# Hidden units and their sums swap storage after the first turn of a Strassen-like MLP, and their stores are split over two stages

## The chip, the cores and the metric

The kernel runs on one core of one Trainium2 chip. The metric is the device time of one execution in microseconds (us), as the median of some runs. All times inside an execution are counted from the start of the profiled span. Engines are called by their profile names: PE (matrix multiply), ACT (scalar engine), DVE (vector engine), POOL (GpSimd) and SP, which here only issues DMAs, in order, from one queue.

## The reference, cut to what matters

The program is one layer of an encoder: a mixer of two attention kinds, a cross-attention, and an MLP with a squared ReLU. Only the MLP is touched here. With 1024 tokens, a model width of 1024 and a hidden width of 4096 it computes

```python
h = h + parallel_mixer(...)
h = h + memory_cross_attention(...)
u = jax.nn.relu(rms_norm(h, norm_mlp_g) @ mlp_w1)    # (1024, 1024) @ (1024, 4096)
h = h + (u * u) @ mlp_w2                              # (1024, 4096) @ (4096, 1024)
```

## The kernel before, in words

All matrix products are in float32 precision: every operand is split into a high part and a low part, and one product is three matmuls (lines L107, L108 and L109, in `gemm`). Inside the MLP the kernel also uses a seven-product scheme for 2x2 block matrices (Winograd's form of Strassen's method): seven block products instead of eight, paid with sums and differences of blocks. A **stage** is one of these seven block products; it is done for two block rows, `i` = 0 and 1, each with 12 matmuls of 128x512 when four 128-deep slices are contracted. So a stage is 24 matmuls.

The MLP has two parts.

The **hidden part** (`mlp`, the loop over `p`) makes the squared units in eight **turns** of seven stages. A turn makes two units groups, q = 2p + i. What a group leaves is eight planes of 128x512: four planes of units, called `c` (c[0] to c[3]), and four planes of sums and differences of them, called `t` (t[0] to t[3]). They live for the length of a turn in the storage of the state `h`, seen as `h4` with four blocks of four planes: `h4[:, 2 + i]` holds `c` and `h4[:, i]` holds `t`. The function `hidden(i, j, ps)` takes the PSUM bank of stage `j`: stages 0 to 2 are copied by ACT (L1151), stages 3 to 5 are added by DVE (L1159). At stage 5 ACT applies ReLU and square to c[0:3] (L1161, L1162) and DVE forms t[0:3] (L1163, L1164); at stage 6 ACT makes c[3] (L1153, L1154) and DVE makes t[3] (L1156). Then two DMAs of 1 MB each store c (L1155) and t (L1157) into `ud[q]` in DRAM, planes 0 to 3 and 4 to 7.

The **output part** (the loop over `CHUNKS`) reads the planes of `nk` groups back from `ud` (L1202), splits them (ACT L1203, DVE L1204), multiplies them with blocks of `w2` and accumulates into `h`, which is free by then. It goes over `o` = 0 and 2: with o = 0 the function `output` writes rows k = 0 to 3 of `h`, which is the storage of `h4` blocks 0 and 1; with o = 2 it writes blocks 2 and 3. In the first chunk the stages j = 0, 2, 3 and 6 are plain copies by ACT (L1228), the others are DVE adds (L1230). A copy may write into `h` only when the DMA that stores the old content of these planes has landed. In the first chunk's seven stages, j = 2 and j = 4 and 6 accumulate in the same PSUM bank as j = 0, and j = 5 in the bank of j = 3, so the matmuls of j = 2 wait until ACT has read the bank of j = 0.

The weights are loaded by `weights7` into a pool `raw7` of two buffers (SP, L1060), split by ACT and DVE (L1039, L1040), and summed into tiles `s` by POOL in the output part (L1065, L1066, L1072, L1073). Names in the traces and listings: `x_1859`, `x_1896`, `x_1860`, `x_1908`, `x_1899`, `x_1909` and `x_1910` are the seven operand tiles of the hidden stages 0 to 6, reused as slots for what the output part reads back; `my`, `mm` and `tr` are PSUM banks; `g` is a split weight.

The order of the instructions on each engine is made by a scheduler when the program is built, from the dependences between tiles and its own estimates. A change of the code in one place can so reorder others.

Of the kernel before, what the change touches and what calls it, by code (L numbers as in the profile page):

```python
# [51 lines left out]
class Layer:  # L52
# [1041 lines left out]
    def mlp(self, mx):  # L1094
        nc = self.nc
# [15 lines left out]
        def prep(*args):  # L1111
            w = self.weights7(*args)
            A = next(w)
            next(w)
            return A
# [25 lines left out]
        h4 = h.rearrange("p k s -> p (k s)").rearrange("p (b c s) -> p b c s", b=4, s=512)  # L1141
        for p in range(NQ // 2):
            if p:
                A = prep([self.w1[2 * p + i] for i in range(2)], 512, nc.vector, True)

            def hidden(i, j, ps):

                c, t, q = h4[:, 2 + i], h4[:, i], 2 * p + i
                v = c[:, (0, 2, 1, 1, 2, 0, 3)[j]]
                if j in (0, 1, 2):  # L1150
                    nc.scalar.activation(v, ps, AF.Copy)  # L1151
                elif j == 6:
                    nc.scalar.activation(v, ps, AF.Relu)  # L1153
                    nc.scalar.activation(v, v, AF.Square)  # L1154
                    nc.sync.dma_start(self.ud[q, :, 0:4, :], c)  # L1155
                    nc.vector.tensor_tensor(t[:, 3], v, t[:, 2], ALU.subtract)  # L1156
                    nc.sync.dma_start(self.ud[q, :, 4:8, :], t)  # L1157
                else:
                    nc.vector.tensor_tensor(v, ps, v, ALU.add)  # L1159
                    if j == 5:  # L1160
                        nc.scalar.activation(c[:, 0:3], c[:, 0:3], AF.Relu)  # L1161
                        nc.scalar.activation(c[:, 0:3], c[:, 0:3], AF.Square)  # L1162
                        nc.vector.tensor_tensor(t[:, 0:2], c[:, 1:3], c[:, 0:2], ALU.subtract)  # L1163
                        nc.vector.tensor_tensor(t[:, 2], c[:, 2], t[:, 0], ALU.subtract)  # L1164

            def taken(i, j, ps):
                hidden(i, j, ps)
                if p == 0 and i == 1:
                    next(turn, None)

            self.products7(self.HIDDEN, A, B, 4, taken)
            if p == 1:

                self.token_squares(0, self.yv[:, 0:4])
                nc.vector.reciprocal(self.yv, self.yv)
                nc.vector.tensor_tensor(self.yv, self.yv, self.hv, ALU.mult)
            if p == 3:
                F = self.T(self.s7, [P, 2, 512], F32, "s7")
                for half in range(2):
                    ps = next(self.banks)  # L1180
                    self.spread(ps, self.smallp, self.yv[:, 4 * half:4 * half + 4])
                    nc.scalar.activation(F[:, half], ps, AF.Copy)
                nc.sync.dma_start(self.fd, F)
# [12 lines left out]
        for nk in CHUNKS:  # L1196
            B = {}
            for names, room, which in groups:
                for q in range(q0, q0 + nk):
                    t = room[q % 4]  # L1200
# [91 lines left out]
```

## Time and profile before

| What | Value |
|---|---|
| median of the runs | 1480.72 us (1478.56, 1480.72, 1490.71) |
| the profiled execution's own time | 1479.95 us |
| its span | 1478.2 us |
| PE busy | 1428.4 us, 97% of the span |
| DVE, ACT, POOL busy | 925.1, 683.1, 431.8 us |
| MLP | about 851 us to the end |
| last hidden turn | about 1120 to 1158 us |

The span is what the trace covers; 1.75 us of the execution's time lie outside of it. The busy share of PE says that it nearly always has a matmul in flight, not that it runs at its peak. What a change can win must therefore be looked for in the places where PE waits.

### The profile page before, as it was taken

The numbers are of one execution on the slowest core, as the hardware profiler recorded it, in microseconds if no ns is written. First come the engines' busy times: TensorE is split into PE (matmuls) and PEld (weight loads), VectorE is DVE, ScalarE is ACT, GpSimd is POOL, SyncE is SP. The second block draws the span as 40 slices with busy tenths as digits, with TensorE's granted clock in tenths as the row PEclk, the third lists the DMA queues.
The fourth block names the chain that finished last, engine by engine and source line by source line (L and its number), as shares of the span: only waits on it lengthen the run. The fifth ranks groups of instructions, "written<-read, shape, count | busy, mean of one in ns | idle before, by whom it ended". The sixth has DMA issues, their size and how long they took to land.

```text
span 1478.2 us, 19169 instructions
## 1 busy us (share of the span) xinstructions
PE 1428.4 (97%) x7058; PEld 1193.7 (81%) x7058; DVE 925.1 (63%) x1323; ACT 683.1 (46%) x1095; POOL 431.8 (29%) x457
## 2 busy tenths in 40 slices
PE   8998999998998998999999999999999899999998
PEld 6777888886887787888888878888888688888886
DVE  4386422427776576666654895647556939688686
ACT  4474332326776555445542264445445626335230
POOL 2157503323473312622212300000000523333454
PEclk9999999999999999999999999999999999999999
DMA  8425530258677642503375114444446827337353
GB/s 269 126 51 124 143 86 1 72 176 249 183 207 200 190 156 72 161 31 114 117 269 191 45 65 171 171 171 185 171 171 234 280 71 240 129 109 232 115 200 114
DMA packets 125118, 223.94 MB, mean 151 GB/s; under 512 B 8384, under 2 KB 66528, under 8 KB 118368
## 3 DMA queue, kind: packets, MB, share of 16 engines
q1 hardware_dynamic: 125024, 222.71, 46.6%
q8 instruction: 56, 0.92, 0.3%
q14 instruction: 38, 0.31, 0.1%
HBM read 150.59 MB, written 72.09 MB: 151 GB/s over the span
## 4 chain that ended last, share of the span: by engine, by line
PE 80%; DMA 8%; DVE 6%; ACT 2%; issue 2%; POOL 1%; SPq 0%; POOLq 0%; ACTq 0%; DVEq 0%
PE mm L107 13%; PE mm L108 13%; PE mm L109 13%; PE my L108 7%; PE my L107 7%; PE my L109 7%; PE tr L108 3%; PE tr L107 3%; PE tr L109 3%; DMA raw<-in_w_in_dram 1%; PE tr L661 1%; DMA raw<-in_xattn_wkv_dram 1%; PE pv L668 1%; PE pv L669 1%; PE s L621 1%
## 5 line engine op out<-in xcount | busy, mean ns | idle before, releaser
L107 PE MATMUL my<-x,g 128*128 128x512 f32 x464 | 181.5, 392 | 6.4 <-ACT h L1228 6.4
L108 PE MATMUL my<-x,g 128*128 128x512 f32 x464 | 181.6, 391 | 1.3 <-DVE x L1040 1.3
L109 PE MATMUL my<-x,g 128*128 128x512 f32 x464 | 181.1, 391 | 0.0
L108 PE MATMUL mm<-wl,xh 128*128 128x512 f32 x320 | 126.0, 395 | 3.6 <-DVE wl L97 3.6
L107 PE MATMUL mm<-wh,xh 128*128 128x512 f32 x320 | 126.9, 399 | 0.8 <-ACT gv L485 0.8
L1040 DVE TENSOR_TENSOR g<-raw,g 128x1024 fp32r<-128x1024 f32 (+3 forms) x72 | 66.9, 931 | 96.7 <-ACT g L1039 96.7
L109 PE MATMUL mm<-wh,xl 128*128 128x512 f32 x320 | 125.8, 394 | 0.0
L1039 ACT ACTIVATE g<-s 128x1024 fp32r<-128x1024 f32 (+1 forms) x72 | 69.0, 963 | 119.4 <-PE my L109 51.5
L1065 POOL TENSOR_TENSOR s<-raw 128x384 f32<-128x384 f32 (+1 forms) x20 | 26.2, 1312 | 298.1 <-DMA raw<-in_mlp_w_dram 268.9
L107 PEld LDWEIGHTS my<-x,g 128*128 128x128 f32 x464 | 87.6, 189 | 25.1 <-ACT h L1228 6.9
L108 PEld LDWEIGHTS my<-x,g 128*128 128x128 f32 x464 | 87.7, 189 | 19.7 <-DVE x L1040 1.7
L109 PEld LDWEIGHTS my<-x,g 128*128 128x128 f32 x464 | 87.6, 189 | 18.4 <-DVE g L1040 0.2
L1039 ACT ACTIVATE g<-raw 128x1024 fp32r<-128x1024 f32 (+3 forms) x72 | 55.4, 773 | 98.6 <-PE my L109 36.2
L1040 DVE TENSOR_TENSOR g<-s,g 128x1024 fp32r<-128x1024 f32 (+1 forms) x72 | 84.8, 1180 | 14.5 <-ACT g L1039 14.4
L632 POOL TENSOR_SCALAR p<-p,rrec 128x128 f32<-128x128 f32 (+3 forms) x64 | 50.6, 793 | 128.0 <-DVE rrec L631 121.7
L107 PE MATMUL mm<-x,g 128*128 128x512 f32 x220 | 85.7, 390 | 0.0
L108 PE MATMUL mm<-x,g 128*128 128x512 f32 x220 | 85.7, 389 | 0.0
L109 PE MATMUL mm<-x,g 128*128 128x512 f32 x220 | 85.6, 389 | 0.0
L109 PE MATMUL tr<-x,g 128*128 128x512 f32 x212 | 82.6, 390 | 0.3 <-DVE g L1040 0.3
L107 PE MATMUL tr<-x,g 128*128 128x512 f32 x212 | 82.5, 389 | 0.0
L108 PE MATMUL tr<-x,g 128*128 128x512 f32 x212 | 82.5, 389 | 0.0
L1204 DVE TENSOR_TENSOR x<-x 128x1024 fp32r<-128x1024 f32 (+1 forms) x64 | 78.6, 1247 | 6.0 <-ACT x L1203 5.8
(313 smaller groups left out, 3764.6 us busy)
## 6 DMA issues: line engine op xcount, KB each, us to landing
ud<-h SPq DMA_DIRECT2D x32, 1024.0 KB
x<-ud SPq DMA_DIRECT2D x48, 512.0 KB
raw<-in_mlp_w_dram SPq DMA_DIRECT2D x20, 1024.0 KB
raw<-in_mlp_w_dram SPq DMA_DIRECT2D x16, 768.0 KB
raw<-in_w_in_dram SPq DMA_DIRECT2D x23, 512.0 KB
raw<-in_xattn_wkv_dram SPq DMA_DIRECT2D x16, 512.0 KB
od<-o SPq DMA_DIRECT2D x32, 256.0 KB
xt<-in_x_dram SPq DMA_DIRECT2D x8, 512.0 KB
```

The costliest lines, as they stand in the source:

```text
L107: mm(ps, lh[k], rh[k], start=start and k == 0, stop=False, **kw)
L108: mm(ps, lh[k], rl[k], start=False, stop=False, **kw)
L109: mm(ps, ll[k], rh[k], start=False, stop=stop and k == n - 1, **kw)
L621: nc.tensor.matmul(ps[:, c], qa[:, ts], ka[:, c], start=True, stop=False)
L632: nc.gpsimd.tensor_scalar(p[:, 0:n], p[:, 0:n], rr, 1.0, ALU.mult, ALU.mult)
L661: nc.tensor.transpose(o, pp[i][:, kb * P:(kb + 1) * P], self.ident)
L668: nc.tensor.matmul(pv, va[:, kb, :], th[:, js], start=kb == 0, stop=False)
L669: nc.tensor.matmul(pv, va[:, kb, :], tl[:, js], start=False, stop=kb == nb - 1)
L1039: self.nc.scalar.activation(hi, src, AF.Copy)
L1040: self.nc.vector.tensor_tensor(lo, src, f(hi), ALU.subtract)
L1065: eng.tensor_tensor(s[:, 0], raw[:, 3], raw[:, 2], ALU.add)
L1204: nc.vector.tensor_tensor(lo, f(lo), f(hi), ALU.subtract)
```

## The change

```diff
             def hidden(i, j, ps):

-                c, t, q = h4[:, 2 + i], h4[:, i], 2 * p + i
+                c, t = (h4[:, b] for b in ((2 + i, i) if p == 0 else (i, 2 + i)))
+                q = 2 * p + i
                 v = c[:, (0, 2, 1, 1, 2, 0, 3)[j]]
                 if j in (0, 1, 2):
                     nc.scalar.activation(v, ps, AF.Copy)
                 elif j == 6:
                     nc.scalar.activation(v, ps, AF.Relu)
                     nc.scalar.activation(v, v, AF.Square)
-                    nc.sync.dma_start(self.ud[q, :, 0:4, :], c)
+                    nc.sync.dma_start(self.ud[q, :, 3, :], v)
                     nc.vector.tensor_tensor(t[:, 3], v, t[:, 2], ALU.subtract)
-                    nc.sync.dma_start(self.ud[q, :, 4:8, :], t)
+                    nc.sync.dma_start(self.ud[q, :, 7, :], t[:, 3])
                 else:
                     nc.vector.tensor_tensor(v, ps, v, ALU.add)
                     if j == 5:
...
                         nc.scalar.activation(c[:, 0:3], c[:, 0:3], AF.Square)
                         nc.vector.tensor_tensor(t[:, 0:2], c[:, 1:3], c[:, 0:2], ALU.subtract)
                         nc.vector.tensor_tensor(t[:, 2], c[:, 2], t[:, 0], ALU.subtract)
+                        for r, src in ((0, c), (4, t)):
+                            nc.sync.dma_start(self.ud[q, :, r:r + 3, :], src[:, 0:3])
```

It does two things. From the second turn on, the units `c` stand in blocks 0 and 1 of the storage and the sums `t` in blocks 2 and 3. And each of the two stores of 1 MB is divided: planes 0 to 2 (768 KB) go out at stage 5, when they are complete, and the last plane (256 KB) at stage 6. Each turn issues eight stores instead of four; the bytes are the same. No arithmetic is added or removed. Lines behind the change are numbered three higher, so the ACT copy L1228 becomes L1231 and L1202 becomes L1205. The new store of three planes is L1167; those of single planes are L1156 (c) and L1158 (t).

The first place is the queue of SP at the end of the last turn. Its rows before, from the load of the third weight block of the output part to the first load of the next chunk; `raw` is a weight buffer, `x` a slot that is filled from `ud`:

```order
L1060 DMA raw_2086_10811<-in_mlp_w_dram 128x4x512
L1202 DMA x_1910_8688<-ud_68 128x512 x2
L1060 DMA raw_2088_10816<-in_mlp_w_dram 128x4x512
L1155 DMA ud_68<-h_5812 128x2048
L1157 DMA ud_68<-h_5812 128x2048
L1155 DMA ud_68<-h_5812 128x2048
L1157 DMA ud_68<-h_5812 128x2048
L1060 DMA raw_2106_11075<-in_mlp_w_dram 128x4x384
```

And now:

```order
L1060 DMA raw_2086_10843<-in_mlp_w_dram 128x4x512
L1205 DMA x_1909_8657<-ud_68 128x2x512 x2
L1167 DMA ud_68<-h_5812 128x1536
L1205 DMA x_1910_8688<-ud_68 128x512 x4
L1167 DMA ud_68<-h_5812 128x1536 x3
L1060 DMA raw_2088_10848<-in_mlp_w_dram 128x4x512
L1156 DMA ud_68<-h_5812 128x512 x2
L1158 DMA ud_68<-h_5812 128x512 x2
L1060 DMA raw_2106_11107<-in_mlp_w_dram 128x4x384
```

The four stores of three planes moved ahead of the load of `raw_2088`, the first of them also ahead of the four loads of `x_1910`; the four stores of one plane stand behind that load, where the whole stores stood. The two loads of `x_1909`, which stood ahead of `raw_2086`, now stand behind it.

The second place is ACT at the start of the output part. `my_2080` and `my_2081` are the banks of stage 0 (and 2) for i = 0 and 1, `tr_2084` and `tr_2085` those of stage 3; the copies L1203 and L1206 split operand slots. Before:

```order
L1203 ACTIVATE x7_1910_8688<-x7_1910_8688 128x512 x2
L1039 ACTIVATE g2_2076_10611<-s7_2074_10605 128x1024
L1039 ACTIVATE g2_2077_10614<-s7_2075_10608 128x1024
L1228 ACTIVATE h_1369_5812<-my_2080_10623 128x512
L1228 ACTIVATE h_1369_5812<-tr_2084_10705 128x512
```

And now:

```order
L1231 ACTIVATE h_1369_5812<-my_2080_10655 128x512
L1206 ACTIVATE x7_1910_8688<-x7_1910_8688 128x512 x4
L1039 ACTIVATE g2_2076_10643<-s7_2074_10637 128x1024
L1039 ACTIVATE g2_2077_10646<-s7_2075_10640 128x1024
L1231 ACTIVATE h_1369_5812<-my_2081_10669 128x512
```

The copy of the bank of stage 0 for i = 0 moved ahead of the splits of `x_1910` and of two weight splits; that for i = 1 stands right behind them.

The third place is PE, where the matmuls of output stage 2 for i = 0 begin. Before, the stages 0, 1 and 3 are all done first, 72 matmuls; the rows around the border:

```order
L108 MATMUL tr_2085_10719<-x7_1908_8628,g2_2073_10602 128x512
L109 MATMUL tr_2085_10719<-x7_1908_8628,g2_2073_10602 128x512
L107 MATMUL my_2080_10623<-x7_1860_8212,g2_2071_10596 128x512
L108 MATMUL my_2080_10623<-x7_1860_8212,g2_2071_10596 128x512
L109 MATMUL my_2080_10623<-x7_1860_8212,g2_2071_10596 128x512
```

And now:

```order
L108 MATMUL tr_2084_10737<-x7_1860_8212,g2_2071_10628 128x512
L109 MATMUL tr_2084_10737<-x7_1860_8212,g2_2071_10628 128x512
L107 MATMUL my_2080_10655<-x7_1860_8212,g2_2071_10628 128x512
L108 MATMUL my_2080_10655<-x7_1860_8212,g2_2071_10628 128x512
L109 MATMUL my_2080_10655<-x7_1860_8212,g2_2071_10628 128x512
```

Stage 2 for i = 0 now begins after 54 matmuls of the output part, in the middle of stage 3 for i = 0, which is 18 matmuls sooner. Behind it come the other six matmuls of that stage, three of stage 3 for i = 1, and then stage 2 for i = 1, so that this begins after 75. Stage 5 for i = 0, the first to use the bank `tr_2084` again, begins after 108.

## The prediction

> **What bounds the kernel now.** I began with the page, then asked who PE waited for in the MLP, then followed the chain of waits there.
>
> ```profile
> span 1478.2 us, 19169 instructions
> ...
> PE 1428.4 (97%) x7058; PEld 1193.7 (81%) x7058; DVE 925.1 (63%) x1323; ACT 683.1 (46%) x1095; POOL 431.8 (29%) x457
> ```
>
> PE is busy for 97% of the span, so a change that adds and removes no matmul can win only where PE stands still. The waits of PE between 850 us and the end (columns: total us, times, longest) are three:
>
> ```profile
> PE my L107 <- ACT h L1228: 6.4, 1, 6.4
> PE my L108 <- DVE x L1040: 1.3, 1, 1.3
> PE tr L109 <- DVE g L1040: 0.3, 1, 0.3
> ```
>
> Only the first is large. The chain of waits (start, length, what) shows what stood behind it:
>
> ```profile
> 1170.68 0.61 DVE h L1156
> 1171.31 9.43 DMA ud<-h
> 1180.83 0.60 ACT h L1228
> 1181.48 0.79 PE my L107
> ```
>
> This is the step from the hidden part to the output part. ACT may not copy output stage 0 into the storage of the state until the sums t of group 14, which lie there, are in DRAM. Their store is issued at 1171.31 and has landed at 1180.7. The timeline of PE shows what that costs:
>
> ```profile
> 1174.65 0.39 PE L109 MATMUL tr<-x,g 128*128 128x512 f32 x1
> 1181.48 0.79 PE L107 MATMUL my<-x,g 128*128 128x512 f32 x1 [6.44 <-ACT h L1228]
> ...
> 1186.51 0.40 PE L107 MATMUL tr<-x,g 128*128 128x512 f32 x1
> ...
> 1188.78 0.39 PE L108 MATMUL tr<-x,g 128*128 128x512 f32 x1
> ```
>
> Undisturbed matmuls start every 0.227 us (ten steps between the last two rows, 2.27 us). The one after 1174.65 should have started at 1174.88 and starts at 1181.48: **6.60 us**. The next 12 then take 1181.48 to 1186.51, 5.03 us instead of 12 x 0.227 = 2.72: another **2.31 us**. The windows give the reason, a granted clock (the figure behind POOL's) of 0.50 after the wait; the last two columns are the share of the DMA engines and GB/s:
>
> ```profile
> 1158.00:1162.00 4.00, 4.00 (x19) 3.22 (x18) 4.00 (x4) 4.00 (x6) 1.91 (x1) 1.00 0.86 249
> 1166.00:1170.00 4.00, 4.00 (x19) 3.32 (x18) 4.00 (x2) 4.00 (x8) 3.00 (x2) 1.00 0.00 0
> 1175.00:1181.00 6.00, 0.04 (x1) 0.00 (x0) 6.00 (x7) 0.17 (x1) 2.43 (x2) 0.86 1.02 431
> 1181.00:1186.00 5.00, 4.52 (x11) 3.56 (x12) 0.69 (x2) 0.92 (x2) 4.83 (x4) 0.50 0.78 328
> ```
>
> The second row is the telling one: from 1166 to 1170 no DMA moves anything, and afterwards they are full. The queue of SP says why:
>
> ```profile
> 1157.70 0.55 SPq L1060 DMA_DIRECT2D raw<-in_mlp_w_dram  x1
> 1158.34 1.04 SPq L1202 DMA_DIRECT2D x<-ud  x2
> 1169.02 0.55 SPq L1060 DMA_DIRECT2D raw<-in_mlp_w_dram  x1
> 1169.67 0.57 SPq L1155 DMA_DIRECT2D ud<-h  x1
> 1171.31 0.32 SPq L1157 DMA_DIRECT2D ud<-h  x1
> 1171.74 0.71 SPq L1155 DMA_DIRECT2D ud<-h  x1
> 1177.56 0.32 SPq L1157 DMA_DIRECT2D ud<-h  x1
> ```
>
> All four stores stand behind a weight load that goes out at 1169.02. POOL holds it, with the last of its sums over the buffer to be reloaded, done at 1168.99:
>
> ```profile
> 1166.71 2.28 POOL L1073 TENSOR_TENSOR s<-raw,s 128x512 f32<-128x512 f32 x1
> ```
>
> Meanwhile the first three planes of the units had long been made (ACT, groups 14 and 15), while the first three planes of group 15's sums were finished late, behind other work of DVE:
>
> ```profile
> 1153.60 1.49 ACT L1162 ACTIVATE h<-h 128x1536 f32<-128x1536 f32 x1
> ...
> 1161.88 1.47 ACT L1162 ACTIVATE h<-h 128x1536 f32<-128x1536 f32 x1
> ```
>
> ```profile
> 1170.01 0.68 DVE L1164 TENSOR_TENSOR h<-h 128x512 f32<-128x512 f32 x1
> ```
>
> **The change, part by part.** *The swap.* Output stage 0 now overwrites the units, which are ready earlier than the sums: 1155.09 for group 14 and 1163.35 for group 15. *The split.* Planes 0 to 2 go out ahead of the late weight load. The first copy needs plane 0 alone, so it waits for the first L1167 only.
>
> When does that store land? At the earliest it is issued when ACT is done, 1155.09; 0.79 MB at 431 GB/s are 1.8 us, so 1156.9. At the latest it goes behind the load at 1157.70 and the two loads of x_1909 that now stand between them. I count these in full: 1.05 + 1.05 + 0.79 = 2.89 MB from 1157.70 on. At 249 GB/s, the rate of the window from 1158 to 1162, that is 11.6 us, so 1169.3; at 431 GB/s it is 6.7 us, so 1164.4. ACT's copy takes 0.60, so the bank is free between 1157.5 and 1169.9. I take some 1165, nearer to the middle, since the earlier stores of the sixth turn also leave less in the queue ahead.
>
> When is it needed? The hidden part ends 71 matmuls and the 0.3 us of the small stall before 1174.65, at 1158.2. Stage 2 for i = 0 now begins after 54 matmuls, 1158.2 + 54 x 0.227 = 1170.5. So even the latest bound is 0.6 us in time, and my value 5 us. For i = 1 ACT has behind the first copy four splits of x_1910, two weight splits and the copy:
>
> ```profile
> 1168.65 1.14 ACT L1203 ACTIVATE x<-x 128x512 fp32r<-128x512 f32 x2
> 1169.69 2.09 ACT L1039 ACTIVATE g<-s 128x1024 fp32r<-128x1024 f32 x2
> ```
>
> That is 2 x 1.14 + 2.09 + 0.60 = 5.0 us, so 1174.9 from the latest bound, and it is needed after 75 matmuls, at 1175.2. Its store, of group 15's units, waits for 1163.35 and moves 0.79 MB behind the 1.05 MB of x_1910: 1.84 MB at 249 GB/s are 7.4 us, so 1170.8.
>
> *The single planes* c[3] stand behind raw_2088, and that now stands behind the sums of group 15, made at 1170.69 in the old order. 0.79 + 1.05 + 0.26 = 2.10 MB then take 4.9 us at 431 GB/s or 8.4 at 249: landed between 1175.6 and 1179.1. Stage 5 for i = 0 needs the copy of stage 3 after 108 matmuls, at 1182.7. This has 3 to 7 us. The sums themselves are now overwritten by o = 2 only, 168 matmuls or 38 us after 1158.2. The weight load raw_2088 may be 2 us later than before; its matmuls begin after 180, at 1199.
>
> *The small stall* of 0.3 us, PE's wait for a weight split on DVE: DVE is behind there, and the operand loads now come earlier, since three quarters of the sixth turn's stores have left. I count it as gone; staying would cost 0.3.
>
> *More DMAs.* Four more issues per turn. A turn's end on SP now looks like this:
>
> ```profile
> 970.76 0.38 SPq L1157 DMA_DIRECT2D ud<-h  x1
> 982.00 0.33 SPq L1060 DMA_DIRECT2D raw<-in_mlp_w_dram  x1
> ```
>
> The next weights go out 11 us after the last store, held by their buffer, so four more issues of 0.3 to 0.9 us are hidden; without that cover they would cost 3 us on that load. In the turns the DMAs have room, and the copies that waited for a store (ACT, 13 times) never held PE:
>
> ```profile
> 889.00:927.00 38.00, 38.00 (x169) 31.48 (x168) 22.18 (x29) 18.66 (x23) 0.00 (x0) 1.00 0.43 166
> ```
>
> ```profile
> ACT h L1151 <- DMA ud<-h: 27.6, 13, 3.4
> ```
>
> With stores at stage 5 those waits only shorten. I cost the turns at nothing; as the other end, 1 us in each of seven turns is 7 us lost.
>
> One rule speaks against the change. The Trainium skill, "DMA: Bandwidth & Descriptors", section "Rules for kernel authors", asks for at least 1 MiB per DMA and to coalesce many small transfers; the change does the opposite. The trace bears out that smaller loads run slower: 249 GB/s around the loads of 256 KB, 431 around whole stores. By that rule the first store lands near 1169.3 in place of 1165, which leaves the sum as it is but little in hand, and speaks for the first rival below.
>
> The sum: 6.60 + 2.31 + 0.3 = **9.2 us** of the profiled execution's 1479.95, so 1470.7, and I say 1471. That execution lies 0.8 us below the median of the runs shown, 1480.72, one of which is 10 us above the others.
>
> **The rivals.** *A part of the wait stays.* If POOL lets raw_2086 go 3 us later, or the loads are slower, the first store lands past 1169.9, and PE waits for the rest. Short waits here also cost clock: earlier in this trace PE waited 1.9 us, and the window behind has a granted clock of 0.59.
>
> ```profile
> PE pv L669 <- DVE ptl L115: 1.9, 1, 1.9
> ```
>
> ```profile
> 554.00:558.00 4.00, 3.78 (x19) 3.32 (x18) 4.00 (x9) 2.56 (x6) 1.17 (x2) 0.59 0.56 193
> ```
>
> A rest of 3 us plus 2 us of half clock leaves 9.2 - 5 = 4 us of gain: 1476. For it: the load stands ahead of the store, and ACT works in order. Against: the latest bound, made of the slowest rate, is still in time. The Trainium skill, "TensorE: Matmul & The Clock Gate", section "Why this matters for your kernels", sets the limit for a clock drop at idle gaps of about 3 us; by it a rest of 2 us would cost no clock and give 1473, while the row with 1.9 us says it may.
>
> *The change does not do what it says.* The stores stay held in SP's queue, or another wait of the same length takes the place, as DVE, 4.00 of 4.00 us busy from 1166 to 1170, is still behind. Then 1480. Against it: neither the first store nor the copy behind it needs DVE's sums.
>
> *Slower.* The single planes c[3] are the place. They stand behind raw_2088, which waits for POOL's sums, for the third store ahead of it and so for DVE. If they land after 1182.1, PE stops at stage 5. From a wait of 9.2 - 2.3 = 6.9 us, that is landing at 1189, 10 us after the slow bound, the kernel is slower than before; a raw_2088 held until 1187 in place of 1171 would land them at some 1194 with the 2.10 MB, a wait of 12 + 2.3 us: 1485. For it: three things in a row that each wait in order. Against: DVE and POOL get their operands earlier, not later.
>
> **How the numbers follow.** Forecast (the wait goes, 1471): 0.67. A part stays (1476): 0.16. No change (1480): 0.08. Slower (1485, with a tail): 0.09. The lower end takes all three waits of PE and the half clock away, 1479.95 - 8.0 - 2.3 = 1469.6, and 1.4 us for runs that differ (1478.56 against 1479.95): 1468. The upper end takes in the cases to no change and a little of the slower one: 1482. About 1%, 14.8 us, is what a measurement of this kernel can tell from no change. A gain above it would need more waits than PE has in the MLP, so faster 0.02; slower by more is the tail of the last rival, 0.04; within 1% 0.94.
>
> **What would show it.** Right: no wait of PE on L1231 near 1170, no window of granted clock 0.50 there, the first L1167 of the last turn issued between 1155 and 1160, DMAs at work between 1166 and 1170, MLP turns still 38 us long. Wrong: PE waiting for L1231 on a bank `my` (first store late) or `tr` (single planes late), or for L1040 inside the turns (weights late), or the granted clock low in another place.

## The result, and the profile after

The changed kernel takes 1476.06 us in the median of 22 runs (1467.45 to 1482.72); the kernel before, in 22 runs beside them, 1484.3 us (1478.56 to 1490.71). The ratio is **0.9947, with a 95% interval from 0.9935 to 0.9959**: a gain of 7.9 us, between 6.1 and 9.6. The profiled execution took 1476.15 us.

The head of its page, span and first section:

```profile
span 1474.3 us, 19250 instructions
...
PE 1427.8 (97%) x7058; PEld 1193.9 (81%) x7058; DVE 927.6 (63%) x1323; ACT 683.4 (46%) x1095; POOL 431.2 (29%) x457
```

The engines' work is what it was; what changed is where PE stands still. Its waits after 850 us:

```profile
PE my L107 <- ACT h L1231: 1.7, 1, 1.7
PE my L108 <- DVE x L1040: 1.3, 1, 1.3
PE my L184 <- DVE dg L183: 1.2, 2, 1.0
```

The 6.4 us before ACT's copy have become 1.7, the small stall on DVE's weight split is gone, and one wait is new, on L184 in a hidden turn. The timeline of PE at the step:

```profile
1173.77 0.39 PE L107 MATMUL my<-x,g 128*128 128x512 f32 x1
...
1178.33 0.39 PE L109 MATMUL tr<-x,g 128*128 128x512 f32 x1
1180.38 0.50 PE L107 MATMUL my<-x,g 128*128 128x512 f32 x1 [1.67 <-ACT h L1231]
...
1183.23 0.39 PE L107 MATMUL tr<-x,g 128*128 128x512 f32 x1
```

Stage 2 for i = 0 begins at 1173.77 without a wait; the wait that is left stands before stage 2 for i = 1. It should have started at 1178.56 and starts at 1180.38, 1.8 us late. The 12 matmuls behind it take 2.85 us, where undisturbed ones take 2.72: no half clock this time. The windows (DMA share and GB/s last, the clock ahead of them) say the same:

```profile
1158.00:1162.00 4.00, 4.00 (x20) 3.30 (x19) 4.00 (x4) 2.74 (x3) 4.00 (x3) 1.00 0.18 46
...
1166.00:1170.00 4.00, 4.00 (x19) 3.30 (x19) 3.97 (x4) 3.64 (x4) 1.02 (x1) 1.00 0.94 344
1175.00:1181.00 6.00, 4.33 (x20) 3.27 (x19) 6.00 (x7) 4.32 (x7) 3.77 (x2) 1.00 1.02 381
1181.00:1186.00 5.00, 5.00 (x24) 4.13 (x23) 5.00 (x7) 1.64 (x3) 1.78 (x2) 1.00 0.69 264
```

The hole in the DMAs from 1166 to 1170, which carried the prediction, is filled. The granted clock is 1.00 in all four. But there is a new hole ahead, from 1158 to 1162. The queue of SP shows it:

```profile
1159.81 0.55 SPq L1060 DMA_DIRECT2D raw<-in_mlp_w_dram  x1
1160.44 1.08 SPq L1205 DMA_DIRECT2D x<-ud  x2
1163.10 0.33 SPq L1167 DMA_DIRECT2D ud<-h  x1
1163.52 2.10 SPq L1205 DMA_DIRECT2D x<-ud  x4
1167.73 4.30 SPq L1167 DMA_DIRECT2D ud<-h  x3
1172.86 0.55 SPq L1060 DMA_DIRECT2D raw<-in_mlp_w_dram  x1
```

The first L1167 goes out at 1163.10, as soon as ACT has made group 14's units. ACT made them late, because it waited 2.44 us for DVE's add at stage 5. DVE made that add at 1158.55, right behind two weight splits; in the kernel before, these two come behind both adds of stage 5 (L1159, at 1151.37 and 1156.44), at 1158.68 and 1161.51. The rows of DVE, then those of ACT:

```profile
1155.21 3.41 DVE L1040 TENSOR_TENSOR g<-raw,g 128x1024 fp32r<-128x1024 f32 x2
1158.55 0.68 DVE L1160 TENSOR_TENSOR h<-my,h 128x512 f32<-128x512 f32 x1
```

```profile
1159.26 1.49 ACT L1162 ACTIVATE h<-h 128x1536 f32<-128x1536 f32 x1 [2.44 <-DVE h L1160]
1160.65 1.04 ACT L1206 ACTIVATE x<-x 128x1024 fp32r<-128x1024 f32 x1
1161.60 1.47 ACT L1163 ACTIVATE h<-h 128x1536 f32<-128x1536 f32 x1
...
1166.72 1.48 ACT L1163 ACTIVATE h<-h 128x1536 f32<-128x1536 f32 x1
...
1172.95 0.58 ACT L1231 ACTIVATE h<-my 128x512 f32<-128x512 f32 x1
...
1179.73 1.09 ACT L1231 ACTIVATE h<-my 128x512 f32<-128x512 f32 x2 [1.68 <-DMA ud<-h]
```

Group 15's units are ready at 1168.20. Their store is issued at 1169.09, when a load of x_1909 has landed, and the chain of waits says how long it then took:

```profile
1160.44 8.58 DMA x<-ud
1169.09 10.56 DMA ud<-h
1179.73 0.61 ACT h L1231
1180.38 0.50 PE my L107
```

10.56 us for 0.79 MB is 75 GB/s, in a stretch in which all DMAs together moved some 380 (381 from 1175 to 1181). It shared the engines with transfers issued beside it, among them the three planes of sums of group 14 (1167.73) and of group 15 (1171.71), which nobody was waiting for.

### The profile page after: what moved, and what is told of

Same layout as the page of the kernel before. It is cut to its first block, busy times and chain, and to the rows that moved or that the text cites. A ratio compares the mean times of both kernels' runs of the same rounds, so it can differ in the third digit from the quotient of the medians.

```text
span 1474.3 us, 19250 instructions
## 1 busy us (share of the span) xinstructions
PE 1427.8 (97%) x7058; PEld 1193.9 (81%) x7058; DVE 927.6 (63%) x1323; ACT 683.4 (46%) x1095; POOL 431.2 (29%) x457
## 4 chain that ended last, share of the span: by engine, by line
PE 66%; issue 16%; DMA 9%; DVE 5%; ACT 2%; POOL 1%; SPq 0%; POOLq 0%; DVEq 0%; ACTq 0%
PE mm L107 12%; PE mm L108 12%; PE mm L109 12%; PE my L108 4%; PE my L107 4%; PE my L109 4%; PE tr L107 2%; PE tr L108 2%; PE tr L109 2%; DMA raw<-in_w_in_dram 2%; PE tr L661 1%; DMA raw<-in_xattn_wkv_dram 1%; PE pv L669 1%; PE pv L668 1%; PE s L621 1%
## 5 line engine op out<-in xcount | busy, mean ns | idle before, releaser
L1040 DVE TENSOR_TENSOR g<-raw,g 128x512 fp32r<-128x512 f32 (+3 forms) x72 | 68.3, 951 | 69.1 <-ACT g L1039 69.0
L1039 ACT ACTIVATE g<-raw 128x512 fp32r<-128x512 f32 (+3 forms) x72 | 55.5, 773 | 101.0 <-DMA raw<-in_mlp_w_dram 39.3
L1040 DVE TENSOR_TENSOR g<-s,g 128x1024 fp32r<-128x1024 f32 (+1 forms) x72 | 86.1, 1199 | 7.7 <-ACT g L1039 7.5
```

Source lines behind the costliest of these rows:

```text
L1039: self.nc.scalar.activation(hi, src, AF.Copy)
L1040: self.nc.vector.tensor_tensor(lo, src, f(hi), ALU.subtract)
```

## The experiments

All times of the MLP in the table are read from the trace: its start is PE's first matmul into a bank `my`, and its length goes from there to the end of the span. "Step" is PE's wait for the copy (L1228 before, L1231 after). A gain in us is worked out from the ratio; plain medians can differ from it by about 1 us.

| kernel | ratio to before (95%) | MLP starts | MLP length | step |
|---|---|---|---|---|
| before, three profiles | | 849.3, 854.4, 856.2 | 628.9, 628.6, 628.6 | 6.4, 6.7, 6.8 |
| whole change, two profiles | 0.9947, 0.9946 | 851.1, 852.1 | 623.2, 623.5 | 1.7, 2.0 |
| split alone, two profiles | 0.9967, 0.9954 | 853.7, 853.3 | 622.6, 623.0 | 1.2, 1.4 |
| swap alone | 0.9983 (0.9968 to 0.9998) | 855.3 | 628.2 | 4.3 |
| swap, units' store split | 0.9940 (0.9919 to 0.9960) | 851.0 | 621.2 | none |
| all turns but the last | 1.0006 (0.9992 to 1.0021) | 852.9 | 629.8 | 6.0 |
| swap, units' store split, spread on POOL | 0.9962 (0.9942 to 0.9983) | 851.2 | 624.1 | none |
| last turn, units' store split | 0.9946 (0.9927 to 0.9964) | 853.3 | 620.3 | none |

**Split alone.** The blocks stay where they were:

```diff
-                c, t = (h4[:, b] for b in ((2 + i, i) if p == 0 else (i, 2 + i)))
+                c, t = h4[:, 2 + i], h4[:, i]
```

> Stores split as in the change, but units and sums keep their old places. The queue of SP has the same order as in the changed kernel. Theory A (both parts are needed): the first ACT copy now waits for the first three planes of the sums of group 14, whose store is issued some 5 us later than that of the units, behind the loads of x_1910; it lands about 4 us too late for PE, PE waits about 4 us for that copy and loses about 2 us more to the half clock. Gain on the kernel before 3 us (1 to 5). Theory B (the split alone does it): no more than the 1.7 us wait of the changed kernel, gain about 8 us. Theory C (the swap alone does it) and theory D (the gain lies in the turns): gain 0 by C, about 8 us by D.

Measured: 1478.88 us, ratio 0.9967 (0.995 to 0.9984), 4.9 us of gain. PE's waits at the step and in the turns:

```profile
PE my L108 <- DVE x L1040: 1.3, 1, 1.3
PE my L184 <- DVE dg L183: 1.2, 2, 1.0
PE my L107 <- ACT h L1231: 1.2, 1, 1.2
```

A is wrong on the mechanism: without the swap the step's wait is 1.2 us, not 4, and there is no half clock. The sums are ready later than the units, but the scheduler answered by putting stage 2 for i = 0 after 68 matmuls of the output part instead of 54, and ACT's copy for it at 1180.16 was nearly in time. The gain of 4.9 us is still inside A's 1 to 5, so the two kernels were measured side by side.

**Whole change and split alone on one chip.**

> The changed kernel itself, on the same chip and in the same rounds as the three kernels that follow, so that they can be compared with it directly. Both theories: 7.9 us faster than before (6.1 to 9.6), a ratio of 0.9947; PE waits 1.7 us for the second copy L1231 and 1.2 us on L184 in a turn, and the granted clock stays at 1.00 behind both.

> The stores divided in all turns, the units and sums not swapped: once more, now beside the whole change. A (the swap is worth something on top of the split): 2 to 4 us slower than the whole change in the same rounds, as the two separate comparisons with before say (4.9 against 7.9 us of gain). B (the split alone is the change): within 1.5 us of it, since both traces show PE waiting the same 1.2 to 1.8 us at the step and 1.2 us on L184, and no half clock.

Measured: the whole change 1476.01 us (1475.23 to 1477.44), ratio 0.9946 (0.9931 to 0.9961); split alone 1478.15 us (1475.55 to 1478.74), ratio 0.9954 (0.9938 to 0.997). The medians differ by 2.1 us, which would be A's, the ratios by 0.0008, which is 1.2 us and would be B's, and the intervals overlap widely; in the MLP itself split alone is the shorter one by 0.5 us. So B stands in the traces, and that the swap is worth anything on top of the split is not shown. The window at the step of this second profile of the whole change, with PE's wait of 2.0 us ending at 1181.63, has a full clock too:

```profile
1181.00:1186.00 5.00, 4.37 (x19) 3.60 (x20) 5.00 (x8) 2.02 (x3) 0.51 (x1) 1.00 0.93 351
```

**Swap alone.** The whole stores at stage 6 come back:

```diff
-                    nc.sync.dma_start(self.ud[q, :, 3, :], v)
+                    nc.sync.dma_start(self.ud[q, :, 0:4, :], c)
...
-                    nc.sync.dma_start(self.ud[q, :, 7, :], t[:, 3])
+                    nc.sync.dma_start(self.ud[q, :, 4:8, :], t)
...
-                        for r, src in ((0, c), (4, t)):
-                            nc.sync.dma_start(self.ud[q, :, r:r + 3, :], src[:, 0:3])
```

> Units and sums swapped after the first turn, but stored whole at the seventh stage. The queue of SP has the same order as in the kernel before. Theory A (both are needed): the store of the units of group 14 still stands behind the weight load held until 1169, but one store of 1 MB ahead of the sums, so it lands 1.05 MB / 0.43 MB per us = 2.4 us sooner; PE still waits about 4 us and has the half clock. Gain on the kernel before 2.4 us (1 to 4). Theory C (the swap alone does it): PE's wait under 2 us, gain about 8 us. Theories B (split alone) and D (turns): gain 0.

Measured: 1481.67 us, ratio 0.9983, 2.5 us of gain, as A said, of which the MLP's length shows 0.5: the step's wait is 2.1 us shorter than in the first profile of before, but a wait for DVE's split (L1040) grows from 0.3 to 0.9 us and the turns are 0.7 us longer. The step keeps its wait and the half clock behind it (waits, the queue of SP, and the window after the step):

```profile
PE my L107 <- ACT h L1229: 4.3, 1, 4.3
```

```profile
1176.29 0.55 SPq L1060 DMA_DIRECT2D raw<-in_mlp_w_dram  x1
1176.93 0.57 SPq L1156 DMA_DIRECT2D ud<-h  x1
```

```profile
1186.00:1192.00 6.00, 5.33 (x13) 4.19 (x14) 2.86 (x3) 1.12 (x3) 4.79 (x4) 0.54 1.02 431
```

The store still goes out right behind the late weight load. Swapping what is waited for helps little while both kinds of planes stand behind the same held load.

**All turns but the last.** Swap and split for p = 1 to 6, split for p = 0, the last turn as before:

```diff
+                split = p < NQ // 2 - 1
+                c, t = (h4[:, b] for b in ((i, 2 + i) if 0 < p < NQ // 2 - 1 else (2 + i, i)))
```

> Swap and split in the turns before the last only; the last turn keeps the old places and whole stores, so the step to the output part is as in the kernel before. Theory A (the gain is all at the step): PE waits 6 to 7 us on the first copy as before and has the half clock; gain 0 (within 1.5 us either way). Theory D (the turns gain): about 8 us.

Measured: 1483.81 us, ratio 1.0006 (0.9992 to 1.0021), with the step back at its old wait:

```profile
PE my L107 <- ACT h L1232: 6.0, 1, 6.0
```

Of the 64 parts into which 32 stores are divided, 56 gain nothing. A holds: the whole gain lies at the one step. The MLP's length is 629.8 against 628.7; the fourth turn (p = 3) is 1.7 us longer, as in the changed kernel, and the step's wait a little shorter.

**Only the units' store divided.** This tests why the second copy was late. The sums of both groups leave whole at stage 6, so they are no longer in the DMA engines beside group 15's units:

```diff
-                    nc.sync.dma_start(self.ud[q, :, 7, :], t[:, 3])
+                    nc.sync.dma_start(self.ud[q, :, 4:8, :], t)
...
-                        for r, src in ((0, c), (4, t)):
+                        for r, src in ((0, c),):
```

> The change, but only the units' store is split; the sums are stored whole at the seventh stage, behind the weight load. Theory A with the rest of the wait put down to the DMA queue (in the changed kernel the units of group 15 land 10.6 us after their issue, with the 0.79 MB of group 14's sums ahead of them): these land 2 us sooner, PE's wait of 1.7 us on L1231 falls under 0.5 us; gain on the kernel before 9 to 10 us, 1.5 us more than the change. Rival: the rest is set by ACT's own order (operand and weight splits ahead of the second copy), then the wait stays between 1.2 and 2 us and the gain is that of the change, 8 us.

Measured: 1474.7 us, ratio 0.9940, 8.9 us of gain, just under A's 9 to 10 and not clear of the changed kernel's 7.9. PE does not wait at the step at all. The rows of the queue and of ACT's copies:

```profile
1169.27 0.32 SPq L1167 DMA_DIRECT2D ud<-h  x1
1173.01 0.55 SPq L1060 DMA_DIRECT2D raw<-in_mlp_w_dram  x1
```

```profile
1172.08 0.59 ACT L1231 ACTIVATE h<-my 128x512 f32<-128x512 f32 x1
1175.84 0.60 ACT L1231 ACTIVATE h<-my 128x512 f32<-128x512 f32 x1
```

The second store is issued at 1169.27, as in the changed kernel (1169.09), and its copy runs at 1175.84 instead of 1179.73. It landed within 6.6 us instead of 10.56. This shows the rest of the wait to be the sums' transfers beside the units'. (Which group's sums did it is not separated. ACT's order changed too, one weight split of about 1 us now stands behind the copy; but in the changed kernel ACT itself stood idle 1.68 us for the store.)

**The spread of the token factors on POOL.** PE's new wait on L184 stands in turn p = 3, where eight 128x128 diagonal tiles `dg` are made and multiplied. Before, the scheduler had set these matmuls in groups between 976 and 1016 us; now DVE makes them behind the sums of a turn's end (L1164, L1157), and the first of PE's matmuls, from 1005.5 to 1008.3, stand close together. The kernel above, with these tiles made by POOL, which is idle there:

```diff
-    def spread(self, ps, pool, col):
+    def spread(self, ps, pool, col, eng=None):
...
-            nc.vector.tensor_scalar(dg, self.ident, col[:, j:j + 1], None, ALU.mult)
+            (eng or nc.vector).tensor_scalar(dg, self.ident, col[:, j:j + 1], None, ALU.mult)
...
-                    self.spread(ps, self.smallp, self.yv[:, 4 * half:4 * half + 4])
+                    self.spread(ps, self.smallp, self.yv[:, 4 * half:4 * half + 4], nc.gpsimd)
```

> Swap, the units' store divided, the sums stored whole at stage 6; and the four diagonal tiles of the token factors, which PE waits for on L184 in turn p = 3, are made by POOL instead of DVE. A (that wait is what the turns lose): PE no longer waits on L183 or L184, the stretch from the first matmul of the MLP to the first of the output part falls from 310.4 to about 309.2 us, and the kernel is 10 us faster than before (8.5 to 11.5). B (the turns lose their time elsewhere, or POOL is busy just then): the stretch stays at 310.4 us or grows, and the gain stays at 8.9 us or less.

Measured: 1477.42 us, ratio 0.9962, 5.6 us of gain: not better. PE's waits, POOL's timeline and the windows at that place:

```profile
PE my L184 <- POOL dg L183: 2.3, 3, 1.1
```

```profile
1006.10 5.39 POOL L183 TENSOR_SCALAR dg<-ident,yv 128x128 f32<-128x128 f32 x5 [69.48 <-PE my L184]
```

```profile
1006.00:1010.00 4.00, 1.74 (x10) 1.15 (x9) 3.90 (x7) 1.65 (x3) 3.90 (x4) 1.00 1.02 411
1010.00:1014.00 4.00, 4.00 (x12) 3.10 (x11) 3.38 (x4) 2.00 (x2) 1.49 (x2) 0.57 1.03 418
```

B holds: the stretch grows from 310.4 to 313.3 us. A is wrong in its remedy: POOL takes 1.08 us for a tile (5.39 / 5) where DVE takes 0.28, PE waits 2.3 us in three pieces instead of 1.2, and a half clock follows. The place is what A named, since a slower maker of `dg` lengthens the wait there; the MLP is 2.9 us longer than with DVE (624.1 against 621.2).

**Only the last turn, only the units' store.**

```diff
+                split = p == NQ // 2 - 1
+                c, t = (h4[:, b] for b in ((i, 2 + i) if split else (2 + i, i)))
...
+                nc.sync.dma_start(*((self.ud[q, :, 3, :], v) if split else (self.ud[q, :, 0:4, :], c)))
...
+                        for r, src in ((0, c),) if split else ():
```

> Swap and divided units' store in the last turn alone, the sums stored whole; the first seven turns are written as before. A (the step alone pays and the turns only lose by their new order): the stretch from the first matmul of the MLP to the first of the output part is 308.7 to 309.4 us as before, PE does not wait on L184, PE does not wait at the step, and the gain is 9 to 11 us. B (the new order of the turns helps the step, by what it leaves in the DMA queues): PE waits 2 us or more at the step again and the gain is 4 to 7 us.

Measured: 1475.38 us, ratio 0.9946, 8.0 us of gain. PE's waits after 845 us:

```profile
PE my L108 <- DVE x L1040: 1.3, 1, 1.3
PE my L109 <- DVE g L1040: 0.5, 1, 0.5
```

Neither L184 nor the step appears. The MLP has 620.3 us, the shortest of all, 8.4 under before. (The hidden part's own length can't be read here, since output stages now stand between its last matmuls.) Its fourth turn takes 39.2 us as before, where the changed kernel's takes 40.9. In its trace A holds: the wait on L184 came from the new order of the turns. Its total stayed 1 us under A's 9 to 11 by the ratio (the medians differ by 9.0) and above B's 4 to 7. Neither this version nor the one with all turns can be told from the changed kernel by the medians; no version run here beats it beyond doubt.

**The kernel before, profiled again.** The gain in the MLP, 628.9 - 623.2 = 5.7 us, is less than the 7.9 of the medians.

> The kernel before, unchanged, profiled a second time. In the first two profiles of the changed kernel the stretch from the first matmul of the MLP to the end takes 623.2 and 623.5 us, in the first of the kernel before 628.9: 5.6 us of gain in the MLP against 7.9 in the medians of all runs. A (the rest is chance of the one profile, whose execution was 4 us under its median): 629 to 630 us again here, with the start of the MLP between 850 and 856 us, where nothing was changed. B (the gain lies wholly in the MLP and the first profile of before is untypical there): 631 us or more here.

> The same a third time, to see how far the two stretches of one kernel differ between executions. A: MLP 629 to 630 us, the part ahead of it anywhere between 850 and 856. B: MLP 631 us or more.

Measured: 1484.75 and 1486.51 us. The MLP takes 628.6 us in both, 0.4 under A's band and nowhere near B's; its start is at 854.4 and 856.2, the last 0.2 above A's band. So the MLP repeats to 0.3 us, and the executions differ ahead of it. The windows from 550 to 580, of the first profile of before, of the second, and of the changed kernel, show the largest piece:

```profile
550.00:580.00 30.00, 24.35 (x163) 21.24 (x163) 24.57 (x48) 20.51 (x44) 5.97 (x8) 0.94 0.21 65
```

```profile
550.00:580.00 30.00, 25.04 (x146) 21.73 (x145) 23.35 (x45) 20.29 (x44) 6.57 (x9) 0.77 0.19 58
```

```profile
550.00:580.00 30.00, 24.42 (x168) 21.32 (x167) 26.00 (x49) 22.01 (x47) 6.73 (x9) 0.94 0.21 64
```

The same matmul of PE starts at 550.08 in the first and 551.39 in the second profile of before, 1.3 us apart; 30 us on it is 580.19 and 585.00, 4.8 us apart. So 3.5 of the 5.2 us between the two starts of the MLP are lost in this stretch. Up to the MLP the kernel before and the changed kernel issue the same instructions in the same order on every engine.

## Why the prediction was right or wrong

**Right: where, and that it is a small gain.** The forecast was 1471 in a range from 1468 to 1482, no difference by more than 1%; measured 1476.06. That this is also the 1476 of the rival "a part of the wait stays" is chance: the rival meant 4 us of gain on 1480, and the runs gave 7.9 on 1484.3. "About 1%" was too wide for what can be told from no change: the interval is 0.12% to either side. The gain is at the step from the hidden part to the output part, it comes from the stores that no longer stand behind the late weight load, and the kernel with all turns but the last shows that nothing else pays.

**Right in its place, wrong in its reason: the swap.** The prediction let the units' earlier readiness carry half of the argument. Split alone takes the step to 1.2 to 1.4 us of wait, swap alone only to 4.3. What decided was the place in SP's queue. The versions without any wait at the step all contain the swap, though; dividing only one of the stores without it was not run.

**Mis-sized: when the first store goes out.** It was to leave between 1155 and 1160, with the copy done 5 us early. The units of group 14 were to be ready 2.9 us ahead of the output part's start (1155.09 against 1157.95); they were ready 1.5 us behind it (1163.07 against 1161.53), since DVE's add at stage 5 had come to stand behind two weight splits. "DVE and POOL get their operands earlier, not later" was not so for this add. The first copy began at 1172.95 and ended 0.2 us ahead of its matmul: in time, with no margin left.

**The step that failed: the second store.** The sum had 7.4 us for it, from the bytes of x_1910 and its own at 249 GB/s. It left out the sums that the same edit puts beside it, 0.79 MB of group 14 ahead and as much of group 15 behind, and started it from 1163.35 where the units came at 1168.20. It took 10.56 us, and the copy came 1.8 us late. That is the rival "a part of the wait stays", but in the second copy, not the first, and without its half clock. Here the Trainium skill's limit for a clock drop, some 3 us of idle time ("TensorE: Matmul & The Clock Gate", "Why this matters for your kernels"), fits the 1.7 us wait at clock 1.00; it does not fit the 1.9 us wait with 0.59 in the prediction. The rate of 249 GB/s, for its part, does not show what smaller loads cost: that window also held the 1 MB load of `raw_2086`, issued at 1157.70.

**Mis-sized: the turns cost 1.7 us, not nothing.** From the MLP's first matmul to the output part's first it is 310.4 us instead of 308.7. The prediction counted DMA issues and queue time; it did not ask which engine's order the scheduler would change in the middle of the turns. Seven of the eight turns are as long as before, to 0.02 us; the fourth takes 40.9 us instead of 39.2. 1.2 us of that is PE's wait on L184; the other 0.5 are not traced to a row.

**The account.** 9.2 us were expected in the MLP. The step gives 9.2 - 1.9 = 7.3, the turns take 1.7 back, together 5.6; the lengths of the MLP say 5.4 (628.7 against 623.3). The medians say 7.9. The other 2.5 us are not in the MLP, as far as these five profiles show, and nothing ahead of it was changed. The forecast's starting point mattered more than either: 1479.95 was an execution that was quick ahead of the MLP, and the median of 22 runs lies 4.4 us above it.

**Still open.** Why executions of the changed kernel are quicker ahead of the MLP by 2 to 3 us in the median. Three profiles of before start the MLP at 849.3 to 856.2, two of after at 851.1 and 852.1. Two of the three lost about 3.5 us more than the first in the stretch from 550 to 580; of the nine profiles of versions with the change or parts of it, one lost about 2 us there, the others nothing. No run here shows why that should depend on the change, and it may be chance: for the other versions the gain by the ratio lies between 1.2 us below and 2.0 us above that of the MLP's length.

The expected marks, by their order: no clock of 0.50 at the step, seen; first L1167 between 1155 and 1160, missed (1163.10); DMAs at work from 1166 to 1170, seen (344 GB/s); turns still 38 us long, true in that seven keep their 38.1 to 39.7 us, but not the fourth; a wait on a bank `my`, the mark of a late store, seen at 1.7 us.

## What to carry to other kernels

When a store is late, look first at what it stands behind in its queue; dividing it so that the finished part goes out ahead of the blocked instruction was worth more here than storing something that is ready sooner. Divide only the store that is waited for: the others, set free at the same moment, shared the DMA engines with it here and cost the 1.8 us that were left in the trace. And where a scheduler sets the order, edit the one turn that matters and look for new waits in the turns that were meant to stay as they are.

## What was not expected of the hardware

The same wait does not always cost clock: 1.9 us near 554 us were followed by a window at 0.59, 1.7 and 2.0 us at the step by 1.00, and waits of 1.15, 0.29 and 0.82 us in a row by 0.57. Where a wait falls seems to matter. In all twelve traces a half clock begins and ends on a grid of 3.41 us that is fixed for the whole execution: in the first profile of before it begins at 554.72 and ends at 558.13, and 183 steps after the first of these it begins again at 1179.36, to end two steps later at 1186.18. The 1.9 us fell into one step of that grid, the 1.7 us of the changed kernel on both sides of a border (before, two steps; changed kernel, two steps):

```profile
551.30:554.70 3.40, 1.49 (x11) 1.31 (x11) 3.40 (x7) 2.63 (x8) 0.00 (x0) 1.00 0.67 206
554.75:558.10 3.35, 3.30 (x13) 3.02 (x14) 3.35 (x8) 1.91 (x4) 1.17 (x2) 0.50 0.52 172
```

```profile
1175.90:1179.30 3.40, 2.81 (x13) 2.00 (x11) 3.40 (x2) 2.15 (x3) 3.06 (x2) 1.00 1.00 369
1179.30:1182.70 3.40, 2.32 (x10) 1.95 (x11) 3.40 (x7) 2.03 (x3) 0.00 (x0) 1.00 1.04 387
```

PE was busy for 1.49 of 3.40 us ahead of the half clock, and for 2.81 and 2.32 where none followed. That is a reading, not a rule: with the tiles on POOL a step with 2.01 us was followed by a half clock, and with only the last turn changed one with 1.58 us (344.90 to 348.30) was not.

And the clock can stay low for very different times in the same instructions: the 30 us from 550 on had a granted clock of 0.94 in one execution and 0.77 in two others of one kernel. PE's waits there were nearly the same (1.9, 1.6 or 1.5, and 0.9 us, but 1.3 against 0.6 us on L621), and the 3.5 us lost are most of the difference between 1479.95 and 1484.75 us.
